# A hybrid encoder layer on one core: another PSUM bank for the first down accumulator, another order of down's first steps, and chunk 0's normalized inputs begun four items earlier

## The chip, the cores and the metric

The kernel runs on one core of one Trainium2 chip. The metric is the device time of one execution in microseconds (us). Engines are named as in the profile: PE (TensorE, matmuls), DVE (VectorE), ACT (ScalarE), POOL (GpSimd) and SP (SyncE, which here issues nearly all DMAs). Each engine has its own queue and works through it in order; between engines the instructions wait for each other by semaphores.

## The reference

One layer of a streaming encoder over 1056 tokens of width 1024 (1024 of a prompt, 32 of a sample). Cut to what matters here:

```python
h = rms_norm(x, g_mix);  z = h @ w_in          # q, k, v, conv and gates
a  = window_attn(q, k, v) @ w_attn_out
bo = (cb * conv) @ w_conv_out
x = x + (sigmoid(ga) * a + sigmoid(gb) * bo) @ w_mix_out
hc = rms_norm(x, g_cross)
co = softmax((hc @ w_cq) @ mem_k * s) @ mem_v   # cross attention, 256 memory tokens
x = x + co @ w_co
hm = rms_norm(x, g_mlp)
x = x + square(relu(hm @ w_up)) @ w_down        # hidden 4096
y = rms_norm(x, g_final)
```

All in float32.

## The kernel before, in words

Activations lie transposed: features on the 128 partitions (eight feature blocks f), tokens along the free axis in three chunks of 384, 384 and 288 tokens (chunks 0, 1, 2). Every float32 matmul is made of three fp32r products of split operands: high part times high part, high times low, low times high. `split` makes the parts: ACT casts the high part (L120), DVE subtracts to get the low part (L121). Where a gain belongs to it, ACT and DVE do it at L256 and L257.

*Weights.* `fetch_w` loads a raw weight tile of 128x1024 with a DMA on SP (L138, `wr`, two buffers), and `issue_w` splits it into `wh` and `wl` (three buffers each); two weights are split ahead of the one in use (`LOOK`). A kept weight has its low part loaded again from DRAM (L149) and only its cast made (L150). A usual item of the program is one weight against one chunk: 24 matmuls (`gemm`, L176 to L178) into one accumulator in PSUM.

*The trunk and what runs beside it.* `trunk(c)` is a list of 16 items of chunk c: eight `do_conv_out(c, f)` (it loads the attention branch from DRAM at L1075 and the gate at L1077, multiplies on DVE at L1080, adds at L1083 on POOL, on DVE for the last f, and splits the sum into M tiles), then eight `do_mix(c, f)` (L1093 loads x, L1097 adds it on DVE and so frees the accumulator). `beside(steps, fillers, late)` interleaves: item i of the fillers, then those of `late` that are due at i, then one step of the cross attention of the chunk before. `cross_steps(1)` are those steps for chunk 1: `do_cq`, then per head `scores` (reduce L1175, reciprocal L1178, scale L1180), `turn` (transposed probabilities, split) and `values` (L1210, L1211, L1217, L1219, L1222, L1223 give the Y tiles that `co` multiplies), then `do_co` in two halves of 24 matmuls each (L1236 to L1238, each result added to x at L1241).

*Normalized MLP inputs.* `normed_split(c, f)` makes the input of the up projection: DVE multiplies x by gain and the reciprocal root R (L1264) into a tile `ct`, SP stores it to DRAM (L1265, `xn_d`), ACT casts the high part (L1267), DVE subtracts the low part (L1268). The two DVE instructions are pinned in the order in which the program has them; others a scheduler orders, engine by engine, when the program is built. `ct` is a ring of six tiles that nearly all loads share. `normed(c, at)` puts the eight f at items at, at+1, ... of the fillers.

*Up and down.* The MLP over chunks 0 and 1 is computed by products over quadrants with sums and differences of operands (names b11, b21, n4, t2 and so on, 16 feature tiles each, stored in DRAM); chunk 2 is computed plainly (h2, two halves of 16 tiles). The last up pair (`up_pair`) ends with `dve.tensor_sub(h21, B, s1)` (L1419), the last read of its accumulator B. `open_down` (L1430 and following) closes the old PSUM pool and opens a new one, `ps2`, with six accumulators `acc` and two `pt` tiles, in the order in which they are first asked for.

`beside_two` runs down's first phase. Each of its steps (j, t) takes one weight: `prod` makes 24 matmuls of 384 columns against eight tiles of b11 into accumulator j, and `two` 24 of 288 columns against eight tiles of h2 into accumulator ("z", j); all in `part` (L1650 to L1652). With t = 0 they are tiles 0 to 7 (Y tiles for both), with t = 1 tiles 8 to 15 (M tiles for b11, H tiles for h2). Four j with two t are eight steps; `pump` loads the next operands between them (ring `ct`) and splits those that were loaded by the call before. `to_x1` (L1640) adds a finished accumulator to x; `refold` (L1479 to L1486) makes operands of later products on DVE.

Of the kernel before, what the change touches and what calls it, by code (L numbers as in the profile page):

```python
# [10 lines left out]
F32 = mybir.dt.float32  # L11
# [7 lines left out]
P = 128  # L19
# [19 lines left out]
def hybrid_step(ctx: ExitStack, tc: tile.TileContext, io):  # L39
# [5 lines left out]
    def nm(s):  # L45
        uid[0] += 1
        return f"{s}_{uid[0]}"

    def opened(name, **kw):
        cm = tc.tile_pool(name=name, **kw)  # L50
        return cm, cm.__enter__()

    def closed(cm):
        cm.__exit__(None, None, None)
# [7 lines left out]
    ps_cm, ps = opened("ps", bufs=1, space=PSUM)  # L62
# [46 lines left out]
    def item(fn, *keys):  # L109
        plan.append((fn, keys))  # L110
        worder.extend(keys)
# [126 lines left out]
    def chunk_stats(c):  # L238
        chunk_col(c)
        chunk_row(c)  # L240
# [1194 lines left out]
    def open_down():  # L1435
        nonlocal ps, n_acc
        closed(L["cm"])
        closed(ps_cm)
        H["pool"] = ctx.enter_context(tc.tile_pool(name="hpool", bufs=16, reuse_waits="tile"))
        ps = ctx.enter_context(tc.tile_pool(name="ps2", bufs=1, space=PSUM, reuse_waits="tile"))  # L1440
        n_acc = 6
        ps.tile([P, 384], F32, tag="pt", bufs=2, name=nm("pt"))

    def hslot(n):
        return H["pool"].tile([P, n], F32R, tag=f"H{n}", name=nm("H"))
# [43 lines left out]
    def cross_steps(c):  # L1489
        units = [Cross(c, h) for h in ([0, 1, 2, 3] if c < 2 else [4, 0, 1, 2, 3])]  # L1490
        nu = len(units)
        steps = [("call", [mem_load] if c == 0 else [mem_load_s])] if c < 2 else []
        steps.append(("call", [lambda: chunk_stats(c)]))
        steps.append(("items", [(do_cq(c, j), ("w_cq", j)) for j in range(2)]))
        for i in range(nu + 2):
            calls = []
            if i < nu:
                calls.append(units[i].scores)
            if 0 <= i - 2 < nu:
                calls.append(units[i - 2].values)  # L1500
            if 0 <= i - 1 < nu:
                calls.append(units[i - 1].turn)
            steps.append(("call", calls))
            if c < 2 and i < nu:
                steps.append(("call", []))
        if c == 1:
            steps.append(("call", []))
        if c == 2:
            steps.append(("call", [open_late]))
            steps.append(("call", []))  # L1510
            steps.append(("call", []))
        steps.append(("items", [(do_co(c, 0), ("w_co", 0))]))
        steps.append(("items", [(do_co(c, 1), ("w_co", 1))]))
        steps.append(("call", [lambda: chunk_stats(c)]))
        return steps

    def beside(steps, fillers, late=()):
        for i, filler in enumerate(fillers):
            item(*filler)
            for x in [x for at, x in late if at == i]:  # L1520
                item(lambda x=x: x())
            if steps:
                kind, what = steps.pop(0)
                for x in what:
                    if kind == "items":
                        item(*x)
                    else:
                        item(lambda x=x: x())
        return steps

    def trunk(c):
        return [(do_conv_out(c, f), ("w_conv_out", f)) for f in range(NF)] + [
            (do_mix(c, f), ("w_mix", f)) for f in range(NF)
        ]
# [4 lines left out]
    left = beside([], trunk(0))  # L1539
    left = beside(cross_steps(0), trunk(1))  # L1540

    normed = lambda c, at: [(at + f, lambda f=f: normed_split(c, f)) for f in range(NF)]
    left = beside(left + cross_steps(1), trunk(2), normed(0, 6))
    left = beside(left + cross_steps(2), up0(0) + up0(1), [(min(f + 1, NF - 1), x) for f, x in normed(1, 0)])
    assert not left
    for j in range(NF):
# [161 lines left out]
    steps = [(j, t) for j in range(4) for t in range(2)]  # L1708
# [13 lines left out]
    def twos(half, t):  # L1722
        return [h2_of(half, k) for k in range(8 * t, 8 * t + 8)]

    def beside_two(w, kind, then, half, f, begin, more=(), each=None):

        for n, (j, t) in enumerate(steps):
            if (j, t) == (3, 1) and more:
                item(lambda: wanted.__setitem__(slice(0, 0), more))

            def fn(ws, j=j, t=t, n=n):
                prod(kind, j, t, then)(ws)
                pump(pace(13 - 2 * n))
                if each:
                    each(n)
                two(half, j, t, f, begin)(ws)
                pump(pace(12 - 2 * n))

            item(fn, ("w_down", w, j, t))

    def alone(w, kind, then, begin=True, end=True, more=None):
        for j, t in steps:
# [6 lines left out]
            if more and (j, t) == (1, 0):  # L1749
                item(lambda: [pump(0), more()])  # L1750

    want(twos(0, 1), ops("b21"))
    beside_two(0, "b11", ((*C12, True, False), (*C21, False, False), (*C22, False, False), (*C11, True, False)), 0, 0, True,
               twos(1, 0), lambda n: n > 3 and refold(n - 4))
    want(twos(1, 1), ops("n4")[4:], ops("n4")[:4])
    beside_two(1, "b21", ((*C11, True, True),), 1, 0, False, each=lambda n: n < 5 and refold(n + 4))
    want(ops("t2"))
# [2 lines left out]
    for n, (j, t) in enumerate(steps):  # L1760
        then = ((*C12, False, False), (*C21, True, False), (*C22, True, False))
# [124 lines left out]
```

## Time and profile before

| | us |
|---|---|
| median of 3 runs | 1790.34 |
| lowest and highest | 1790.26, 1791.42 |
| the profiled execution itself | 1788.14 |
| its span, first to last instruction | 1786.3 |
| granted TensorE clock, mean | 0.992 of full |

A line of the timeline reads: start, duration, engine, line of the kernel, operation, out<-in by the names of tiles (without buffer numbers), shape, count of equal instructions in a row; in brackets how long the engine was idle before it and whose end released it. PE's weight load overlaps its matmuls (PEld). Matmuls are pipelined, so the distance of two starts is the cost of one, not the duration shown. A row of windows has the busy time of each engine in that stretch, and at the end the granted clock, the DMA engines' mean busy share and the GB/s moved.

### The profile page before, as it was taken

Reading aid. Unit: us, or ns where it says so; the run is one execution under the profiler, and the core shown is the slowest. Engines: PE = TensorE matmul, PEld = TensorE weight load, DVE = VectorE, ACT = ScalarE, POOL = GpSimd, SP = SyncE. Lnnn points to the kernel's source line nnn. Section 1 sums busy time; section 2 is a strip of 40 time slices with the busy share of each in tenths; the row PEclk is TensorE's granted clock in tenths of the full one; section 3 lists DMA queues with packets and bytes.
Section 4 is the critical chain, followed back from the end, with each engine's and each line's share of the span. In section 5 each row is a group of like instructions: output and inputs, shape, how many; then the busy total and the mean of one; then the engine's idle time right before and its main releaser. Section 6 shows DMA issues by size and latency. Waiting matters only on the chain.

```text
span 1786.3 us, 30138 instructions
## 1 busy us (share of the span) xinstructions
PE 1744.9 (98%) x11030; PEld 1722.1 (96%) x11030; DVE 1195.2 (67%) x2082; ACT 816.3 (46%) x1574; POOL 738.3 (41%) x777
## 2 busy tenths in 40 slices
PE   9999999999999999999999999999999899999997
PEld 8999999999999999999999989999999899999997
DVE  6767696767687767367666877776666666436674
ACT  8655565555332335144465755632222343324453
POOL 2256877874676744402324242375555300100112
PEclk9999999999999999999999999999999999999998
DMA  4424342424332437779766767744334596546672
GB/s 181 144 66 142 100 153 101 146 92 156 120 100 91 161 104 254 262 247 316 261 216 212 248 211 234 264 158 146 138 127 140 161 302 208 166 135 197 194 256 99
DMA packets 177973, 313.04 MB, mean 175 GB/s; under 512 B 18048, under 2 KB 137632, under 8 KB 177696
## 3 DMA queue, kind: packets, MB, share of 16 engines
q1 hardware_dynamic: 168176, 276.97, 46.8%
q0 software_dynamic: 9216, 33.56, 5.3%
q8 instruction: 87, 1.43, 0.3%
q14 instruction: 62, 0.51, 0.1%
q10 hardware_dynamic: 432, 0.58, 0.1%
HBM read 233.23 MB, written 77.81 MB: 174 GB/s over the span
## 4 chain that ended last, share of the span: by engine, by line
PE 81%; DMA 7%; DVE 5%; issue 3%; ACT 2%; POOL 2%; SPq 1%; POOLq 0%; DVEq 0%; ACTq 0%
PE acc L176 10%; PE acc L177 10%; PE acc L178 10%; PE acc L852 6%; PE acc L854 6%; PE acc L853 6%; PE acc L1651 5%; PE acc L1650 5%; PE acc L1652 5%; PE pa L177 2%; PE pa L176 2%; PE pa L178 2%; PE pt L577 2%; DVE wl L121 1%; PE sc L552 1%
## 5 line engine op out<-in xcount | busy, mean ns | idle before, releaser
L121 DVE TENSOR_TENSOR wl<-wr,wh 128x1024 fp32r<-128x1024 f32 (+1 forms) x224 | 313.6, 1401 | 102.5 <-ACT wh L120 101.2
L120 ACT CAST wh<-wr 128x1024 fp32r<-128x1024 f32 (+1 forms) x224 | 234.3, 1046 | 299.0 <-PE acc L1651 73.9
L253 POOL TENSOR_TENSOR xacc<-xacc,ct 128x384 f32<-128x384 f32 (+1 forms) x62 | 76.2, 1230 | 328.3 <-ACT ct L251 325.8
L176 PE MATMUL acc<-X,wh 128*128 128x384 f32 (+1 forms) x624 | 205.1, 329 | 0.6 <-ACT wh L120 0.6
L178 PE MATMUL acc<-Y,wl 128*128 128x384 f32 (+1 forms) x624 | 201.9, 324 | 1.8 <-DVE wl L121 1.8
L178 PE MATMUL acc<-X,wl 128*128 128x384 f32 (+1 forms) x624 | 203.3, 326 | 0.0
L177 PE MATMUL acc<-X,wh 128*128 128x384 f32 (+1 forms) x624 | 202.8, 325 | 0.4 <-DVE X L257 0.4
L176 PE MATMUL acc<-Y,wh 128*128 128x384 f32 (+1 forms) x624 | 202.0, 324 | 1.0 <-DVE ct L1024 0.7
L177 PE MATMUL acc<-Y,wh 128*128 128x384 f32 (+1 forms) x624 | 201.6, 324 | 0.0
L569 POOL TENSOR_SCALAR S<-S,rec 128x256 f32<-128x256 f32 (+1 forms) x132 | 124.8, 959 | 49.8 <-DVE rec L567 49.5
L1650 PE MATMUL acc<-Y,wh 128*128 128x384 f32 (+1 forms) x352 | 114.1, 324 | 6.5 <-DVE lt L1419 6.1
L177 PEld LDWEIGHTS acc<-X,wh 128*128 128x128 f32 x624 | 118.2, 189 | 2.3 <-DVE X L257 1.5
L176 PEld LDWEIGHTS acc<-X,wh 128*128 128x128 f32 x624 | 118.2, 189 | 2.1 <-ACT wh L120 0.8
L178 PEld LDWEIGHTS acc<-Y,wl 128*128 128x128 f32 x624 | 117.1, 188 | 3.1 <-DVE wl L121 3.1
L178 PEld LDWEIGHTS acc<-X,wl 128*128 128x128 f32 x624 | 118.1, 189 | 1.0 <-DVE wl L121 0.2
L176 PEld LDWEIGHTS acc<-Y,wh 128*128 128x128 f32 x624 | 117.0, 188 | 2.1 <-DVE ct L1024 1.0
L177 PEld LDWEIGHTS acc<-Y,wh 128*128 128x128 f32 x624 | 117.1, 188 | 0.0
L1651 PE MATMUL acc<-Y,wh 128*128 128x384 f32 (+1 forms) x352 | 113.9, 323 | 0.1
L1652 PE MATMUL acc<-Y,wl 128*128 128x384 f32 (+1 forms) x352 | 113.7, 323 | 0.0
L120 ACT CAST wh<-s 128x1024 fp32r<-128x1024 f32 x50 | 52.3, 1051 | 89.0 <-PE acc L853 52.2
L121 DVE TENSOR_TENSOR Y<-ct,Y 128x384 fp32r<-128x384 f32 (+1 forms) x128 | 70.7, 581 | 32.6 <-ACT Y L120 32.5
L120 ACT CAST Y<-ct 128x384 fp32r<-128x384 f32 (+1 forms) x128 | 59.6, 486 | 62.7 <-DMA ct<-bc_d 15.2
(359 smaller groups left out, 5231.5 us busy)
## 6 DMA issues: line engine op xcount, KB each, us to landing
wr<-in_w_in SPq DMA_DIRECT2D x55, 512.0 KB, 3.3
wr<-in_w_up SPq DMA_DIRECT2D x48, 512.0 KB, 3.8
wr<-in_w_down SPq DMA_DIRECT2D x32, 512.0 KB, 3.7
wr<-wsum_d SPq DMA_DIRECT2D x32, 512.0 KB, 3.5
wl<-wl_d SPq DMA_DIRECT2D x28, 512.0 KB, 4.7
wr<-in_w_conv_out SPq DMA_DIRECT2D x24, 512.0 KB, 4.9
wr<-in_w_mix SPq DMA_DIRECT2D x24, 512.0 KB, 4.5
xacc<-in_w_down POOLq DMA_DIRECT2D x20, 512.0 KB, 3.8
```

The lines of the kernel that those rows point to most:

```text
L120: act.copy(hi, src)
L121: dve.tensor_sub(lo, src, hi.bitcast(F32))
L176: pe.matmul(out, wh[:, a], hi, start=(k == 0), stop=False)
L177: pe.matmul(out, wh[:, a], lo, start=False, stop=False)
L178: pe.matmul(out, wl[:, a], hi, start=False, stop=(k == len(acts) - 1))
L569: pool_e.tensor_scalar_mul(stl[:, h, :nk], stl[:, h, :nk], rec[:, h : h + 1])
L852: pe.matmul(acc, wh[:, a], hi, start=(start and k == 0), stop=False, skip_group_check=True)
L853: pe.matmul(acc, wh[:, a], lo, start=False, stop=False, skip_group_check=True)
L854: pe.matmul(acc, wl[:, a], hi, start=False, stop=(k == 3), skip_group_check=True)
L1650: pe.matmul(a, wh[:, s], hi, start=(start and k == 0), stop=False, skip_group_check=True)
L1651: pe.matmul(a, wh[:, s], lo, start=False, stop=False, skip_group_check=True)
L1652: pe.matmul(a, wl[:, s], hi, start=False, stop=(stop and k == len(acts) - 1), skip_group_check=True)
```

## The change

Three edits.

1. `open_down` no longer asks for a `pt` tile first. So the accumulators come first in the new pool: the first one takes the bank that the old `pt` tile had (its last reader is L1292 on DVE), and no longer that of the last up pair's B. The third one takes B's.
2. The first `beside_two` gets its own list of steps: (0,0), (1,0), (0,1), (1,1) and then the rest as before. The second step so multiplies the second weight by the tiles that the first step has used, and M and H tiles come in at the third.
3. `normed(0, 6)` becomes `normed(0, 2)`: the eight `normed_split(0, f)` are issued beside items 2 to 9 of `trunk(2)` and not beside 6 to 13.

```diff
@@ open_down
         ps = ctx.enter_context(tc.tile_pool(name="ps2", bufs=1, space=PSUM, reuse_waits="tile"))
         n_acc = 6
-        ps.tile([P, 384], F32, tag="pt", bufs=2, name=nm("pt"))
@@
     normed = lambda c, at: [(at + f, lambda f=f: normed_split(c, f)) for f in range(NF)]
-    left = beside(left + cross_steps(1), trunk(2), normed(0, 6))
+    left = beside(left + cross_steps(1), trunk(2), normed(0, 2))
@@
-    def beside_two(w, kind, then, half, f, begin, more=(), each=None):
+    def beside_two(w, kind, then, half, f, begin, more=(), each=None, steps=steps):
         for n, (j, t) in enumerate(steps):
@@
     beside_two(0, "b11", ((*C12, True, False), (*C21, False, False), (*C22, False, False), (*C11, True, False)), 0, 0, True,
-               twos(1, 0), lambda n: n > 3 and refold(n - 4))
+               twos(1, 0), lambda n: n > 3 and refold(n - 4), [(0, 0), (1, 0), (0, 1), (1, 1)] + steps[4:])
```

Behind L1441 every line of the changed kernel stands one lower: its L1649 to L1651 are L1650 to L1652 of before, its L1639 is L1640, its L1485 is L1486.

Numbers behind a tile's name count buffers. PE's queue where the first step of down ends and the second begins, before (acc_3125 is the first z accumulator, wh_3077 the second weight, M tiles are b11 8 and following):

```order
L1650 MATMUL acc_3125_16442<-Y2_3086_16315,wh_3062_16254 128x288
L1651 MATMUL acc_3125_16442<-Y2_3087_16316,wh_3062_16254 128x288
L1652 MATMUL acc_3125_16442<-Y2_3086_16315,wl_3063_16255 128x288
L1650 MATMUL acc_3112_16393<-M_3099_16358,wh_3077_16296 128x384
L1651 MATMUL acc_3112_16393<-M_3100_16359,wh_3077_16296 128x384
L1652 MATMUL acc_3112_16393<-M_3099_16358,wl_3078_16297 128x384
```

The same place in the changed kernel:

```order
L1649 MATMUL acc_3124_16441<-Y2_3086_16315,wh_3062_16254 128x288
L1650 MATMUL acc_3124_16441<-Y2_3087_16316,wh_3062_16254 128x288
L1651 MATMUL acc_3124_16441<-Y2_3086_16315,wl_3063_16255 128x288
L1649 MATMUL acc_3140_16496<-Y0_3013_16023,wh_3077_16296 128x384
L1650 MATMUL acc_3140_16496<-Y0_3014_16024,wh_3077_16296 128x384
L1651 MATMUL acc_3140_16496<-Y0_3013_16023,wl_3078_16297 128x384
```

The second weight now meets b11 0 (Y0_3013 and its low part Y0_3014) in a third accumulator, where it met b11 8 (M_3099) in the first.

DVE's queue some 20 us later in the same phase, before: splits of the last h2 tiles (H, 128x288), a `refold` (L1486) and the low part of the fourth weight (wl_3140).

```order
L121 TENSOR_TENSOR H_3144_16530<-ct_3135_16485,H_3143_16529 128x288
L1486 TENSOR_TENSOR fold_3196_16780<-fold_3195_16778,fold_3196_16780 128x384
L121 TENSOR_TENSOR wl_3140_16494<-wr_3138_16491,wh_3139_16493 128x1024
L121 TENSOR_TENSOR H_3146_16534<-ct_3136_16487,H_3145_16533 128x288
L121 TENSOR_TENSOR H_3148_16538<-ct_3137_16489,H_3147_16537 128x288
```

And in the changed kernel:

```order
L121 TENSOR_TENSOR H_3144_16526<-ct_3134_16484,H_3143_16525 128x288
L1485 TENSOR_TENSOR fold_3195_16779<-fold_3194_16777,fold_3195_16779 128x384
L121 TENSOR_TENSOR H_3146_16530<-ct_3135_16486,H_3145_16529 128x288
L121 TENSOR_TENSOR wl_3139_16493<-wr_3137_16490,wh_3138_16492 128x1024
L121 TENSOR_TENSOR H_3148_16534<-ct_3136_16488,H_3147_16533 128x288
```

The fourth weight moved behind the seventh H tile and ahead of the eighth; on ACT its cast moved in the same way.

DVE's queue just ahead of co of chunk 1, before (L1264 and L1268 are `normed_split`, L1223 the last value that co waits for, L1241 the first additions of co's results):

```order
L1264 SCALAR_TENSOR_TENSOR ct_2253_11960<-Gb0_1765_9912,prm_72,R_2040_11076 128x384
L1211 TENSOR_TENSOR tO_2257_11972<-o_2256_11967,tO_2257_11972 64x384
L1097 TENSOR_TENSOR Gb2_2276_12061<-acc_2275_12036,xt_2274_12034 128x288
L257 SCALAR_TENSOR_TENSOR Y2_2266_12015<-Gb2_2264_12012,prm_72,Y2_2265_12014 128x288
L1264 SCALAR_TENSOR_TENSOR ct_2268_12021<-Gb0_1774_9954,prm_72,R_2040_11076 128x384
L1268 TENSOR_TENSOR Y0_2255_11964<-ct_2253_11960,Y0_2254_11963 128x384
L1223 TENSOR_TENSOR Y1_2166_11624<-tO_2257_11972,h0_2258_11976 64x384
L257 SCALAR_TENSOR_TENSOR Y2_2278_12064<-Gb2_2276_12061,prm_72,Y2_2277_12063 128x288
L1268 TENSOR_TENSOR Y0_2270_12025<-ct_2268_12021,Y0_2269_12024 128x384
L1241 TENSOR_TENSOR Ga1_1921_10574<-acc_2283_12076,Ga1_1921_10574 128x384
```

The same place in the changed kernel:

```order
L121 TENSOR_TENSOR wl_2264_11989<-wr_2262_11986,wh_2263_11988 128x1024
L257 SCALAR_TENSOR_TENSOR Y2_2257_11968<-Gb2_2255_11965,prm_72,Y2_2256_11967 128x288
L1211 TENSOR_TENSOR tO_2260_11979<-o_2259_11974,tO_2260_11979 64x384
L1097 TENSOR_TENSOR Gb2_2267_12019<-acc_2266_11994,xt_2265_11992 128x288
L1223 TENSOR_TENSOR Y1_2178_11652<-tO_2260_11979,h0_2261_11983 64x384
L1097 TENSOR_TENSOR Gb2_2276_12061<-acc_2275_12036,xt_2274_12034 128x288
L257 SCALAR_TENSOR_TENSOR Y2_2269_12022<-Gb2_2267_12019,prm_72,Y2_2268_12021 128x288
L257 SCALAR_TENSOR_TENSOR Y2_2278_12064<-Gb2_2276_12061,prm_72,Y2_2277_12063 128x288
L1241 TENSOR_TENSOR Ga1_1921_10574<-acc_2283_12076,Ga1_1921_10574 128x384
```

No `normed_split` row stands between the last values and the first addition of co any more; the last two stand ahead of the last two weights of the stretch.

## The prediction

> **What bounds the kernel now.** I read the page first.
>
> ```profile
> span 1786.3 us, 30138 instructions
> PE 1744.9 (98%) x11030; PEld 1722.1 (96%) x11030; DVE 1195.2 (67%) x2082; ACT 816.3 (46%) x1574; POOL 738.3 (41%) x777
> ```
>
> TensorE (PE) is busy 98% of the span. The matmuls themselves are not touched by the change, so it can gain only where PE stands idle or runs at a lowered clock. The second view is the list of PE's waits, sorted by their total (total, times, longest).
>
> ```profile
> PE acc L1650 <- DVE lt L1419: 6.1, 1, 6.1
> ...
> PE acc L1236 <- DVE Gb L1097: 1.6, 2, 1.4
> PE acc L1236 <- ACT Y L1217: 1.6, 2, 0.9
> ...
> PE acc L1651 <- DVE M L121: 0.5, 1, 0.5
> ```
>
> The longest wait of the kernel is the first matmul of the down projection. It waits for L1419, VectorE's last read of accumulator B, and no operand of it comes from there: it is a wait for a PSUM bank. The next place is co, the output projection of the cross attention (L1236). The changed lines touch both. Third, the timeline of PE at the start of down (start, duration, then the wait in brackets):
>
> ```profile
> 1424.43 0.34 PE L854 MATMUL acc<-Y,wl 128*128 128x384 f32 x1
> 1430.92 0.66 PE L1650 MATMUL acc<-Y,wh 128*128 128x384 f32 x1 [6.15 <-DVE lt L1419]
> ...
> 1435.19 0.34 PE L1651 MATMUL acc<-Y,wh 128*128 128x384 f32 x1
> ...
> 1440.30 0.34 PE L1650 MATMUL acc<-M,wh 128*128 128x384 f32 x1
> ...
> 1444.46 0.29 PE L1650 MATMUL acc<-H,wh 128*128 128x288 f32 x1
> ...
> 1447.66 0.34 PE L1650 MATMUL acc<-Y,wh 128*128 128x384 f32 x1
> ```
>
> From these rows: 24 matmuls of 384 columns take 4.16 us (0.173 each, 1440.30 to 1444.46), 24 of 288 take 3.20 (0.133 each), one step of down 7.36. The last matmul before down has its slot until 1424.60, so 1430.92 − 1424.60 = 6.32 us are empty. After that the clock is low: 13 spacings from 1430.92 to 1435.19 take 4.27 us where 13 × 0.173 = 2.25 would do, so 2.0 more are lost. Together 8.3 us.
>
> Fourth, windows of 10 us around co (busy us of PE, weight load, DVE, ACT, POOL, each with its count, then granted PE clock, DMA share, GB/s), and PE's timeline there:
>
> ```profile
> 980.00:990.00 10.00, 10.00 (x73) 10.00 (x72) 7.09 (x12) 7.41 (x13) 1.61 (x2) 1.00 0.76 241
> 990.00:1000.00 10.00, 10.00 (x79) 10.00 (x78) 6.89 (x17) 6.69 (x17) 2.31 (x3) 1.00 0.76 245
> ...
> 1020.00:1030.00 10.00, 9.81 (x72) 9.48 (x71) 10.00 (x18) 7.32 (x14) 4.46 (x3) 1.00 0.83 267
> 1030.00:1040.00 10.00, 7.84 (x27) 6.00 (x27) 8.36 (x14) 5.96 (x11) 7.66 (x8) 0.66 0.70 227
> ```
>
> ```profile
> 1028.90 0.33 PE L1236 MATMUL acc<-Y,wh 128*128 128x384 f32 x1
> ...
> 1031.97 0.44 PE L1236 MATMUL acc<-Y,wh 128*128 128x384 f32 x1 [1.41 <-DVE Gb L1097]
> ...
> 1033.57 1.33 PE L1236 MATMUL acc<-Y,wh 128*128 128x384 f32 x3 [0.61 <-ACT Y L1217]
> ...
> 1039.33 0.29 PE L176 MATMUL acc<-M,wh 128*128 128x288 f32 x1
> ...
> 1042.49 0.34 PE L1236 MATMUL acc<-Y,wh 128*128 128x384 f32 x1
> ...
> 1047.55 0.34 PE L176 MATMUL acc<-Y,wh 128*128 128x384 f32 x1
> ```
>
> Here DVE is the limit: full from 1020 to 1030, while it had about 3 us in 10 free from 980 to 1000. The first 24 matmuls of co take 1039.33 − 1028.90 = 10.43 us where 24 × 0.173 = 4.15 would do: 6.3 lost, partly at a granted clock of 0.66. The second 24 take 5.06: 0.9 lost.
>
> **The change part by part.** *Accumulator bank.* Removing the dummy `pt` tile puts the first accumulator of down on the bank that the old `pt` had. The timeline of DVE there:
>
> ```profile
> 1422.28 0.45 DVE L1292 SCALAR_TENSOR_TENSOR ct<-pa,R 128x288 f32<-128x288 f32 x1
> ...
> 1425.87 1.22 DVE L121 TENSOR_TENSOR wl<-wr,wh 128x1024 fp32r<-128x1024 f32 x1
> ...
> 1427.48 2.36 DVE L121 TENSOR_TENSOR Y<-ct,Y 128x288 fp32r<-128x288 f32 x4
> ...
> 1430.23 0.54 DVE L1419 TENSOR_TENSOR lt<-acc,s 128x384 f32<-128x384 f32 x1
> ...
> 1437.14 1.65 DVE L121 TENSOR_TENSOR M<-ct,M 128x384 fp32r<-128x384 f32 x3 [0.39 <-ACT M L120]
> ...
> 1444.79 1.22 DVE L121 TENSOR_TENSOR wl<-wr,wh 128x1024 fp32r<-128x1024 f32 x1
> 1445.93 1.75 DVE L121 TENSOR_TENSOR H<-ct,H 128x288 fp32r<-128x288 f32 x4
> ```
>
> The old bank is read last by L1292, until 1422.73, before PE needs it. So the first step can start at 1424.6 and end at 1432.0, all in full clock. Its second half, with h2 0–7 (Y, 288 columns), starts at 1428.8; the eighth of these is needed after 21 more spacings, 1428.8 + 21 × 0.133 = 1431.6, and its low part ends at 1429.84: in time. B's bank now belongs to the third accumulator, wanted at 1432.0; L1419 ends at 1430.77. If L1419 were 2 us later, the same wait would return there, shorter.
>
> *Step order.* With the bank alone, PE would come to b11 8–15 (M) at 1432.0, whose last low part ends at 1437.14 + 1.65 = 1438.8: some 6 us of waiting back. The new second step (1,0) takes the operands that are already there and the weight split at 1425.87–1427.1. It runs 1432.0 to 1439.3, and covers the loads of M. M then runs 1439.3 to 1443.5, and h2 8–15 (H) from there, the eighth wanted at 1443.5 + 21 × 0.133 = 1446.3. The timeline of ACT:
>
> ```profile
> 1442.53 1.04 ACT L120 CAST wh<-wr 128x1024 fp32r<-128x1024 f32 x1
> 1444.66 1.90 ACT L120 CAST H<-ct 128x288 fp32r<-128x288 f32 x4 [1.09 <-DMA ct<-hid_d]
> ```
>
> The seventh and eighth H come at 1444.66, released by their load. In the new order the fourth weight's cast (1.04) stands between them on ACT, and its DVE part (1.22) ahead of the eighth's low part: 1444.66 + 0.47 + 1.04 + 0.47 = 1446.6 for the cast, then the weight's low part until 1447.4 or so, then 0.44 more: about 1447.8, a stall of about 1.3 us behind 1446.3 that was not there before. Bounds: 0 if the loads come earlier, 2.5 if the load is as late and the weight also waits. The fifth and sixth weights have lost two steps' slack in part; I take 0.5 for them, 0 to 1.5. Sum of both edits: −8.3 + 1.3 + 0.5 = **−6.5** (−4.3 to −8.3).
>
> What a short stall costs beside itself: after 6.15 us of idling PE was slow for 4.27 us; in co, where no gap was longer than 1.41, the granted clock was 0.66 as well. So a leftover stall of 1.3 may bring up to the same 2.0 of slow matmuls; with it the lower end is −2.3. The Trainium skill, "TensorE: Matmul & The Clock Gate", Part 1, says that the clock drops only after an idle window of about 3.4 us and comes back after about as much sustained work; the 6.15 us case agrees with it, the co rows do not, and by it the stall would cost its own 1.3 alone.
>
> *Chunk 0's normalized MLP inputs earlier, `normed(0, 2)` for `normed(0, 6)`.* Each of eight blocks is a DVE multiply (L1264), an ACT cast (L1267), a DVE subtraction (L1268) and a store on SP (L1265). No work is added; six blocks move ahead of the mix phase, into the stretch where DVE had 3 of 10 us free. The late rows of DVE before:
>
> ```profile
> 1030.06 1.02 DVE L1264 SCALAR_TENSOR_TENSOR ct<-Gb,prm,R 128x384 f32<-128x384 f32 x1
> ...
> 1032.27 0.60 DVE L1264 SCALAR_TENSOR_TENSOR ct<-Gb,prm,R 128x384 f32<-128x384 f32 x1
> 1032.80 1.01 DVE L1268 TENSOR_TENSOR Y<-ct,Y 128x384 fp32r<-128x384 f32 x1
> 1034.08 0.80 DVE L1223 TENSOR_TENSOR Y<-tO,h 64x384 fp32r<-64x384 f32 x1 [0.28 <-ACT h L1222]
> ...
> 1035.65 1.15 DVE L1268 TENSOR_TENSOR Y<-ct,Y 128x384 fp32r<-128x384 f32 x1
> ```
>
> 1.02 + 0.60 + 1.01 + 1.15 = 3.8 us of DVE go from between the last operations that co waits for (L1097, L1223). Of co's 6.3 lost, 2.0 are the two waits named above; most of the rest is slow clock that follows from them. If L1223 comes 2.6 earlier (three rows stand ahead of it) and the clock stays up, 2.6 plus some 2 to 3 of slow matmuls go: −5. The 0.9 of the second 24 stays. Against it stands the load of the conv branch, whose tile ring the new blocks share:
>
> ```profile
> 1004.59 0.46 DVE L1083 TENSOR_TENSOR sgl<-sgl,ct 128x288 f32<-128x288 f32 x1 [0.16 <-DMA ct<-m_d]
> ```
>
> That load now comes later in SP's queue; L1083 may wait 0 to 2 us on DVE, with the queue of DVE behind it, and PE has the mix matmuls' first blocks to cover that. I count it in the range: **−5** (−1 to −7).
>
> Sum: −6.5 − 5 = −11.5. The profiled execution took 1788.14, 2.2 below the median of the runs shown; it becomes 1776.6, and the median 1790.34 becomes 1778.8. Both gains last, since PE is the bound on both sides of each place.
>
> **The rivals.**
>
> *DVE only shifts its delay.* DVE's queue is in order, and the stretch from 980 to 1036 is not empty. If the early blocks push softmax and M splits back, co waits as before and B gives −1.5: −8, 1782.3. For it: DVE full at 1020–1030. Against it: the 3 free us in 10 before 1000.
>
> *Down is bound by its loads.*
>
> ```profile
> 1430.00:1440.00 10.00, 9.08 (x46) 9.12 (x47) 5.98 (x12) 4.13 (x9) 1.00 (x1) 0.74 0.99 337
> ```
>
> The DMA share is 0.99 there. M, H and the weights then come no earlier than before, PE waits at later steps for what it ran ahead of, and the 8.3 shrinks to 3: −8, 1782.3. For it: the casts wait for loads. Against it: in the list of waits down has, beside the first, none over 0.5 us, so there is slack to eat.
>
> *The bank wait changes its name.* Some other thing of the first step (a weight, an operand) holds PE till about 1430: only −5, 1785.3. Against it: the weight and Y rows above.
>
> *Slower: stores in SP's queue.* All eight stores wait in the same in-order queue as the weight fetches.
>
> ```profile
> L1265 SPq DMA_DIRECT2D xn_d<-ct x8: 319/326/422, 1001.6 to 1033.4; - x8
> ...
> DMA to landing us min/median/max: 1.8/4.5/5.8
> ```
>
> A store cannot be issued before its L1264 is done; what stands behind it, the fetch of the next mix weight, waits too. If the six moved stores each held a weight 2 us or more beyond PE's slack, 6 × 2 = 12 us would come on the path and B's −5 be lost: 12 − 6.5 = +5.5, 1795.8. It decides from 6.5 / 6 = 1.1 us each. Against it: an issue takes 0.33 us, and two weights are split ahead of use.
>
> **How the numbers follow.** Forecast as summed 0.52, DVE shift 0.20, loads 0.15, bank wait renamed 0.06, stores 0.05, and 0.02 for no gain at all. The predicted time is 1778.8. The range must reach from −15.3 (both ends of the bounds, 1775.0, and 1 for the spread of 1.2 us among the runs shown) to the case of the renamed wait: 1774 to 1786. Faster or slower counts from 0.2% (3.6 us), about what a measurement of this kernel can tell from no change. Faster: nearly all of the first four cases, 0.88; same: their low ends and the last, 0.07; slower: 0.05.
>
> **What would show it.** Right: the 6.1 us wait for L1419 is gone, the second step starts near 7.4 us after the first, a wait of 1 to 2 us for an H or a weight stands some 20 us into down; the first 24 co matmuls take 5 to 6 us with the granted clock near 1.0 in that window, and DVE is busier from 980 to 1000. Wrong: PE waits for M, H or weights of more than 4 us in down; co still starting with waits for L1097 or L1217 and a clock of 0.66; or waits for weights at L176 between 1000 and 1030.

## The result and the profile after

| | median us (runs) | lowest to highest |
|---|---|---|
| before | 1791.32 (5) | 1790.26 to 1795.09 |
| changed | 1785.37 (5) | 1782.46 to 1787.10 |

The ratio is 0.9963, 95% interval [0.9948, 0.9979]: 0.37% faster, some 6.5 us by the means and 5.95 by the medians. The direction and the range held; 11.5 us had been forecast, and 1785.37 lies 0.6 us inside the slow end of 1774 to 1786. One execution of a later experiment (e7, 2854.96 us) stands far above all others and is left out of its ratio. The profiled execution of the changed kernel took 1785.85 us, with this span:

```profile
span 1784.1 us, 30120 instructions
PE 1744.3 (98%) x11030; PEld 1721.8 (97%) x11030; DVE 1195.0 (67%) x2082; ACT 814.3 (46%) x1574; POOL 735.1 (41%) x777
```

PE's list of waits after (total, times, longest):

```profile
PE acc L1651 <- DVE wl L121: 2.0, 3, 0.8
...
PE acc L176 <- ACT M L120: 1.1, 1, 1.1
PE acc L1236 <- DVE Ga L1241: 1.1, 2, 0.9
...
PE acc L1650 <- DVE H L121: 0.9, 1, 0.9
```

The wait of 6.1 us for L1419 and the waits of co for L1097 are gone. New are short waits for weight low parts (L1651 here is L1652 of before), for an H tile, for an M tile and, where 0.2 us stood before, for L1241's Ga. In PE's timeline at the start of down:

```profile
1426.61 0.34 PE L854 MATMUL acc<-Y,wl 128*128 128x384 f32 x1
1426.79 0.33 PE L1649 MATMUL acc<-Y,wh 128*128 128x384 f32 x1
...
1449.73 0.40 PE L1650 MATMUL acc<-H,wh 128*128 128x288 f32 x1 [0.90 <-DVE H L121]
...
1458.66 0.44 PE L1651 MATMUL acc<-Y,wl 128*128 128x384 f32 x1 [0.64 <-DVE wl L121]
...
1481.68 0.44 PE L1651 MATMUL acc<-M,wl 128*128 128x384 f32 x1 [0.56 <-DVE wl L121]
...
1490.11 0.45 PE L1651 MATMUL acc<-H,wl 128*128 128x384 f32 x1 [0.78 <-DVE wl L121]
```

Down follows up without a gap, but it starts at 1426.8, not at 1424.6: the changed kernel is 2.2 us *later* there. That comes from before any changed instruction. So the two spans cannot be subtracted; the executions are compared stretch by stretch. The borders are the starts of matmuls that all kernels have: the last of co of chunk 0 (L1238), the last of co of chunk 1, the last of up (L854) and PE's last. Ahead of the first border nothing is changed.

| stretch, us | before | changed |
|---|---|---|
| start to co of chunk 0 | 958.2 | 960.5 |
| to co of chunk 1 (edit 3 acts here) | 89.2 | 87.6 |
| to the last matmul of up | 377.1 | 378.5 |
| to PE's last matmul (edits 1, 2) | 353.9 | 349.5 |

So edit 3's stretch gave 1.5 us and down 4.4 in this pair of traces; the first row's 2.3 against it is no work of the change.

Inside the two stretches I count PE's lost time: the distance of each two starts, less 0.173 us for a matmul of 384 columns and 0.133 for one of 288. Between the two co, 8.9 us were lost before and 7.4 after. In the 18 us of co (65 to 83 us behind the border) the loss fell from 6.2 to 1.9, and in the 25 us ahead of it, where conv_out ends and mix begins, it rose from 0.5 to 3.2. PE's timeline has the new waits there:

```profile
1008.58 0.54 PE L176 MATMUL acc<-M,wh 128*128 128x288 f32 x2 [1.10 <-ACT M L120]
...
1019.93 0.40 PE L176 MATMUL acc<-M,wh 128*128 128x288 f32 x1 [0.39 <-ACT wh L150]
...
1031.76 0.45 PE L1236 MATMUL acc<-Y,wh 128*128 128x384 f32 x1 [0.62 <-ACT wh L120]
...
1038.96 0.44 PE L1236 MATMUL acc<-Y,wh 128*128 128x384 f32 x1 [0.90 <-DVE Ga L1241]
```

The windows over co show that the clock stayed up after (1.00, where 0.66 stood before):

```profile
1020.00:1030.00 10.00, 10.00 (x75) 9.97 (x76) 9.79 (x17) 7.43 (x13) 5.64 (x5) 1.00 0.82 271
1030.00:1040.00 10.00, 8.48 (x55) 7.93 (x54) 8.70 (x14) 6.91 (x12) 7.44 (x6) 1.00 0.79 278
```

Why co waits less shows on ACT. L1217 makes a Y tile of co from DVE's sum (L1211). ACT's timeline, before and then in the changed kernel:

```profile
1031.93 1.05 ACT L150 CAST wh<-wr 128x1024 fp32r<-128x1024 f32 x1 [0.30 <-DMA wr<-in_w_co]
1033.01 0.51 ACT L1217 CAST Y<-tO 64x384 fp32r<-64x384 f32 x1
```
```profile
1034.21 0.51 ACT L1217 CAST Y<-tO 64x384 fp32r<-64x384 f32 x1 [1.50 <-DVE tO L1211]
...
1035.16 1.04 ACT L150 CAST wh<-wr 128x1024 fp32r<-128x1024 f32 x1
```

Before, L1217 stands in ACT's queue behind the cast of a kept weight (L150), which waits for its load, and starts 1.5 us after the end of L1211. In the changed kernel it stands ahead of that cast and starts at once. L1211 itself ends no earlier: 73.3 us behind the border before, 73.7 after. PE's order has moved too: in the changed kernel 22 matmuls of a mix item (2.9 us) stand behind co's first two, where before all 24 of co's first half stand in a row.

### The profile page after: what moved, and what is told of

The parts are those of the page before. It is cut to its first block, busy times and chain, and to the rows that moved or that the text cites. A ratio compares the mean times of both kernels' runs of the same rounds, so it can differ in the third digit from the quotient of the medians.

```text
span 1784.1 us, 30120 instructions
## 1 busy us (share of the span) xinstructions
PE 1744.3 (98%) x11030; PEld 1721.8 (97%) x11030; DVE 1195.0 (67%) x2082; ACT 814.3 (46%) x1574; POOL 735.1 (41%) x777
## 4 chain that ended last, share of the span: by engine, by line
PE 76%; DMA 9%; DVE 5%; ACT 3%; issue 3%; POOL 2%; SPq 1%; POOLq 0%; DVEq 0%; ACTq 0%
PE acc L176 10%; PE acc L177 10%; PE acc L178 10%; PE acc L852 6%; PE acc L854 6%; PE acc L853 6%; PE acc L1651 4%; PE acc L1650 4%; PE acc L1649 4%; PE pa L177 2%; PE pa L176 2%; PE pa L178 2%; DVE wl L121 2%; PE pt L577 2%; ACT wh L120 1%
## 5 line engine op out<-in xcount | busy, mean ns | idle before, releaser
L176 PE MATMUL acc<-X,wh 128*128 128x384 f32 (+1 forms) x624 | 205.2, 329 | 1.0 <-ACT wh L120 1.0
L176 PE MATMUL acc<-Y,wh 128*128 128x384 f32 (+1 forms) x624 | 202.5, 325 | 2.7 <-DVE ct L1292 1.8
L176 PEld LDWEIGHTS acc<-Y,wh 128*128 128x128 f32 x624 | 117.7, 189 | 3.6 <-DVE ct L1292 2.0
L176 PEld LDWEIGHTS acc<-X,wh 128*128 128x128 f32 x624 | 118.2, 189 | 2.5 <-ACT wh L120 1.2
L1651 PE MATMUL acc<-Y,wl 128*128 128x384 f32 (+1 forms) x352 | 113.1, 321 | 0.6 <-DVE wl L121 0.6
L1650 PE MATMUL acc<-Y,wh 128*128 128x384 f32 (+1 forms) x352 | 113.1, 321 | 0.2 <-DVE Y L121 0.2
L1649 PE MATMUL acc<-Y,wh 128*128 128x384 f32 (+1 forms) x352 | 113.1, 321 | 0.0
L121 DVE TENSOR_TENSOR Y<-ct,Y 128x384 fp32r<-128x384 f32 (+1 forms) x128 | 71.1, 585 | 28.4 <-ACT Y L120 28.1
```

The lines of the kernel that those rows point to most:

```text
L121: dve.tensor_sub(lo, src, hi.bitcast(F32))
L176: pe.matmul(out, wh[:, a], hi, start=(k == 0), stop=False)
L1649: pe.matmul(a, wh[:, s], hi, start=(start and k == 0), stop=False, skip_group_check=True)
L1650: pe.matmul(a, wh[:, s], lo, start=False, stop=False, skip_group_check=True)
L1651: pe.matmul(a, wl[:, s], hi, start=False, stop=(stop and k == len(acts) - 1), skip_group_check=True)
```

## The experiments

All ratios are to the kernel before, in runs on the same chip (e1 to e4 on one, e5 to e8, e9 to e11 and e12 on three others); "lost" is PE's lost time as above, from one profile each.

| kernel | ratio, 95% interval | co to co, us (lost) | last of up to PE's last, us (lost in its first 95) |
|---|---|---|---|
| before | 1 | 89.2 (8.9) | 353.9 (8.4) |
| changed | 0.9963 [0.9948, 0.9979] | 87.6 (7.4) | 349.5 (4.1) |
| e1, edit 1 | 0.9992 [0.9981, 1.0003] | 88.5 (8.2) | 354.7 (9.4) |
| e2, edit 2 | 1.0005 [0.9995, 1.0015] | 89.7 (9.5) | 353.0 (8.1) |
| e3, edits 1, 2 | 0.9964 [0.9952, 0.9976] | 90.2 (10.0) | 349.3 (3.2) |
| e4, edit 3 | 0.9994 [0.9985, 1.0002] | 87.9 (7.7) | 354.8 (8.8) |
| e5, three steps ahead | 0.9974 [0.9963, 0.9984] | 90.5 (10.3) | 348.3 (3.2) |
| e6, own ring | 0.9967 [0.9955, 0.9980] | 86.1 (5.8) | 350.1 (3.9) |
| e7, stores on ACT | 0.9964 [0.9952, 0.9975] | 87.0 (6.7) | 351.1 (5.6) |
| e8, start 4 | 0.9983 [0.9974, 0.9993] | 93.2 (13.0) | 349.2 (3.1) |
| e9, no fold loads | 0.9968 [0.9955, 0.9981] | 89.9 (9.7) | 346.3 (0.5) |
| e10, ring and ACT | 0.9973 [0.9963, 0.9983] | 87.1 (6.9) | 350.5 (5.0) |
| e11, changed again | 0.9968 [0.9955, 0.9981] | 87.6 (7.4) | 352.4 (5.1) |
| e12, start 3 | 0.9951 [0.9936, 0.9966] | 86.4 (6.2) | 349.1 (3.0) |

**e1, the bank alone.**

```diff
-        ps.tile([P, 384], F32, tag="pt", bufs=2, name=nm("pt"))
```

> Edit 1 alone (first down accumulator on the old pt bank; steps and normed as before). Theory, the bank and the step order work only together: the 6.1 us wait for L1419 is gone, but PE then meets M and H tiles that are no earlier than before; the last H low part of the second step was done at about 1446.8 in the trace of before and PE ended that step at 1447.7, so 0.5 to 1.5 us are gained and waits of some 6 us for M and H tiles stand in the second step. Rival, the bank wait alone was the loss: 6 to 8 us faster, no wait of over 1 us in the second step.

No difference that can be told. The wait for L1419 is gone, and PE meets late tiles in the second step instead. Its timeline in that step (not all waits), and two windows (PE, weight load, DVE, ACT, POOL; then the granted clock):

```profile
1435.05 0.44 PE L1649 MATMUL acc<-M,wh 128*128 128x384 f32 x1 [1.13 <-ACT M L120]
...
1444.72 0.40 PE L1649 MATMUL acc<-H,wh 128*128 128x288 f32 x1 [0.53 <-ACT H L120]
1445.98 0.40 PE L1650 MATMUL acc<-H,wh 128*128 128x288 f32 x1 [0.86 <-DVE H L121]
```

```profile
1430.00:1440.00 10.00, 8.38 (x39) 6.55 (x38) 5.46 (x11) 3.55 (x7) 0.99 (x1) 0.87 0.94 313
1440.00:1450.00 10.00, 8.46 (x39) 7.15 (x38) 7.62 (x15) 7.32 (x14) 0.00 (x0) 0.84 0.93 285
```

The waits with a name come to 3.0 us, but 9.4 are lost: between them PE runs at the pace of the tiles, and at a lowered clock. The theory holds in the main, though less of the loss has a name than the 6 us it expected; the rival that the bank alone was the loss falls.

**e2, the step order alone.**

```diff
-               twos(1, 0), lambda n: n > 3 and refold(n - 4))
+               twos(1, 0), lambda n: n > 3 and refold(n - 4), [(0, 0), (1, 0), (0, 1), (1, 1)] + steps[4:])
```

> Edit 2 alone (down's first steps (0,0), (1,0), (0,1), (1,1); bank and normed as before). Theory, the two work only together: PE still waits about 6 us for L1419, and the new order covers loads that were in time anyway: no difference within 1 us. Rival, the loads of M and H were a limit by themselves: 2 to 4 us faster.

No difference, and the old wait at the head of the list of waits:

```profile
PE acc L1650 <- DVE lt L1419: 6.1, 1, 6.1
```

**e3, both.** The edits of e1 and e2, `normed(0, 6)` as before.

> Edits 1 and 2 without edit 3. Theory, what the changed kernel gained comes from here: about 4 us faster (8.3 us of wait and slow clock gone, some 3 to 4 us of new short waits for H and for weight low parts in down's first eight steps). The sum of the prediction: 6.5 us faster. Rival, the gain is edit 3's: no more than 2 us.

0.9964, as much as the whole change. Neither edit gives anything measurable by itself, together they give nearly all: one takes the wait away, the other what would come in its place. PE's waits with a name from 1420 to 1510 us are three, 1.6 of the 3.2 us lost there:

```profile
PE acc L1650 <- DVE H L121: 0.9, 1, 0.9
PE acc L1649 <- ACT Y L120: 0.4, 1, 0.4
PE acc L1651 <- DVE wl L121: 0.3, 1, 0.3
```

The H here is one at 1503.8, far behind the start; at 22 us into down, where the changed kernel waited 0.9 for an H tile, e3 waits for nothing.

**e4, the normalized inputs alone.**

```diff
-    left = beside(left + cross_steps(1), trunk(2), normed(0, 6))
+    left = beside(left + cross_steps(1), trunk(2), normed(0, 2))
```

> Edit 3 alone (normed(0, 2)). Theory from the trace of the changed kernel: the stretch from the first co of chunk 0 to 1073 us was 1.8 us shorter, since the clock stayed up in co but new waits for M (1.1), for weights (0.4 and 0.6) and for L1241 (0.9) came; so 0 to 2 us faster. The sum of the prediction: 5 us faster, with no such new waits. Rival, the stores in SP's queue hold up weights and the conv branch's load: as slow as before or up to 2 us slower.

In the time, 0.06% with an interval across 1. In the trace, 1.3 us in its stretch, with the same new waits as in the changed kernel:

```profile
1010.43 0.54 PE L176 MATMUL acc<-M,wh 128*128 128x288 f32 x2 [0.60 <-ACT M L120]
...
1041.36 0.44 PE L1236 MATMUL acc<-Y,wh 128*128 128x384 f32 x1 [1.05 <-DVE Ga L1241]
```

And a surprise in the built order. ACT's queue at the fourth weight of down, with edit 3 alone and with edits 1 and 2 alone:

```
edit 3 alone                                      edits 1 and 2 alone
H_3141_16525<-ct_3134_16483 128x288               H_3141_16521<-ct_3133_16482 128x288
H_3143_16529<-ct_3135_16485 128x288               H_3143_16525<-ct_3134_16484 128x288
H_3145_16533<-ct_3136_16487 128x288               wh_3138_16492<-wr_3137_16490 128x1024
wh_3139_16493<-wr_3138_16491 128x1024             H_3145_16529<-ct_3135_16486 128x288
H_3147_16537<-ct_3137_16489 128x288               H_3147_16533<-ct_3136_16488 128x288
```

The weight behind the seventh H tile comes with edit 3, whose instructions stand 400 us earlier, and not with the order of the steps: an edit there has reordered a queue here. It is this form of edit 3 that does it: the traces of e6, e10 and e11 have the order of the left column, those of e7, e8 and e12 that of the right.

**e5, one more step ahead** (edits 1 and 2, edit 3 left out).

```diff
+    [(0, 0), (1, 0), (2, 0), (0, 1), (1, 1), (2, 1)] + steps[6:]
```

> Edits 1 and 2 with one more step ahead, edit 3 left out: (0,0), (1,0), (2,0), (0,1), (1,1), (2,1), then the rest. From the last matmul of up to PE's last, 353.0 to 354.8 us passed without both edits and 349.3 to 349.5 with both. Theory, the rest of the 8.3 us is lost in waits for tiles and weights that are loaded late: one more step on loaded tiles puts M and H 7.4 us later, so no wait for H is left, waits for weight low parts of about 0.5 to 0.9 remain, and the stretch is 348 to 349 us, the whole 0.5 to 1 us faster than edits 1 and 2. Rival, the loads are only moved and PE waits as much for weights instead: 349 to 350, no difference from edits 1 and 2. Slower if the third z accumulator finds its bank held: one new wait in the third step, 350 to 352.

The stretch is 348.3, as the theory had it, but 3.2 us are lost in its first 95 us as in e3, a wait of 0.8 for an H tile stays, and the time is not below e3's. The 1.0 us less than e3 lies behind the 95 us, in the scatter that e11 shows. So the rival is nearer: the loss is only moved.

**e6 to e8** ask what the new wait for an M tile is.

```diff
 e6, normed_split (chunk 0)
-        t = tmp(CH[c][1])
+        t = cr.tile([P, CH[c][1]], F32, tag="nt", bufs=1, name=nm("nt"))
 e7, normed_split (chunk 0)
-        sp.dma_start(xn_d[c][:, f], t)
+        act.dma_start(xn_d[c][:, f], t)
 e8
-    ... normed(0, 2))
+    ... normed(0, 4))
```

> All three edits, and the eight normed_split tiles of chunk 0 in a ring of their own (one buffer) instead of the shared ring ct. From the last co matmul of chunk 0 to that of chunk 1 88.5 to 90.2 us passed in four traces without edit 3, 87.6 and 87.9 with it. Theory, the shared ring holds back the conv branch's loads, which is the new wait for an M tile (1.1 and 0.6 us): it is gone here, and the stretch is 86.3 to 87.0. Rival, the stores in SP's queue hold them back: the wait for M stays. Against it could work that one buffer makes the multiply of the next block wait for the landing of the store before: then DVE has new waits of 1 to 4 us in the conv phase and the stretch is 87.5 or more.

> All three edits, and the eight stores of chunk 0's normalized inputs issued from ACT's queue instead of SP's. Rival theory, SP's in-order queue: the stores hold weight fetches and the conv branch's loads, so the new waits for M (1.1, 0.6) and for the kept weight's cast (0.4) go, and the stretch from co of chunk 0 to co of chunk 1 is 86 to 87 us. Ring theory: the load still waits for its tile in ct, the wait for M stays within 0.5 to 1.2 and the stretch is 87.4 to 88.2.

> All three edits with normed(0, 4) instead of normed(0, 2). Theory, a trade between two losses: two blocks more are left in the mix phase, so co loses more (2 to 4 us after its first matmul instead of 2.0), while the conv branch's loads come two items earlier and the wait for M (1.1) goes: the stretch stays at 87 to 88.5, the whole as with all three edits within 1 us. Rival, the co wait falls away as soon as the last block stands ahead of the last mix weights: 86 to 87, 1 us faster.

In e6 and in e7 the wait for M is gone; in e7 that for the kept weight grew from 0.4 to 0.9, and e6 has a new one of 0.5 for DVE (L1180). What POOL waited for the conv branch's loads (L1083, from 980 to 1012 us) tells more than PE does; the list of waits of before, of the changed kernel, of e7 and of e6:

```profile
POOL sgl L1083 <- DMA ct<-m_d: 5.5, 1, 5.5
```
```profile
POOL sgl L1083 <- DMA ct<-m_d: 29.8, 5, 8.8
```
```profile
POOL sgl L1083 <- DMA ct<-m_d: 24.8, 4, 9.2
```
```profile
POOL sgl L1083 <- DMA ct<-m_d: 16.4, 2, 9.3
```

POOL is not what bounds here (41% busy); the lists show what came last for it. With the stores off SP's queue the loads are hardly earlier: the last is issued 42.3 us behind the border, 43.5 in the changed kernel (40.8 before). With a ring of their own it is issued at 28.1. So the shared ring of six spaces the loads, as the theory had it; that e7 lost the wait for M all the same was not what the theory expected, and what of it is due to the queue and what to loads that landed sooner (at most 5.1 us, 6.2 in the changed kernel) stays open. Neither is faster in the time than the changed kernel.

In e8 the theory of a trade fell: two items later is not as good but much worse, 93.2 us. Co waits in one place longer than before the change, and ACT's timeline has why:

```profile
PE acc L1236 <- ACT Y L1217: 4.0, 1, 4.0
```
```profile
1040.32 1.04 ACT L150 CAST wh<-wr 128x1024 fp32r<-128x1024 f32 x1 [3.45 <-DMA wr<-in_w_co]
...
1041.82 0.51 ACT L1217 CAST Y<-tO 64x384 fp32r<-64x384 f32 x1
```

It is the order of before, with L1217 behind the kept weight's cast, and here that cast waits 3.45 us for its load. The traces without edit 3 have it as well: e1, e2, e3, e5 and e9 wait 1.87, 2.80, 0.68, 2.85 and 3.25 us for L1217, which starts 1.4 to 3.9 us after the end of L1211; with start 2 and 3 in the shared ring and the stores on SP (changed, e4, e11, e12) it starts within 0.6, and PE waits for it in none.

**e9, fewer transfers in down** (edits 1 and 2; the kernel leaves out refold's sixteen loads and fills their tiles with zeros, so some of down's operands hold no data).

```diff
-                    sp.dma_start(fold[k], op_d[k][:, step // 2])
+                    pool_e.memset(fold[k], 0.0)
```

> Edits 1 and 2 without edit 3, and the sixteen loads of refold (192 KB each, 3.1 of the 19.5 MB that move from 1430 to 1500 us) left out: its tiles are set to zero on POOL, so 16 of the 64 sum operands of down are wrong. DVE's subtractions and the stores stay. In the first 95 us from the last matmul of up, 3.15 us are lost in the kernel with edits 1 and 2 (8.4 before), nearly all between 52 and 76 us. Theory, down is now bound there by its transfers: with 16% fewer bytes in that stretch most of the loss goes, 0.3 to 1.2 us are left, and the stretch from the last matmul of up to PE's last matmul is 346 to 348 us (349.3 with edits 1 and 2). Rival, DVE's queue (the subtractions ahead of the weight's low part) or the order of the queues: 2.5 to 3.5 us stay lost, 349 to 350.

0.5 us are lost in the first 95 us of down, where e3 loses 3.2. The ratio, 0.9968, is no better than e3's: in the time the 3 us don't show. The windows from 1480 to 1510 of e3 and then of e9:

```profile
1480.00:1490.00 10.00, 9.72 (x61) 9.40 (x62) 6.59 (x13) 1.05 (x1) 0.00 (x0) 1.00 0.68 216
1490.00:1500.00 10.00, 9.50 (x59) 9.06 (x58) 7.38 (x17) 3.00 (x7) 0.00 (x0) 1.00 0.85 275
1500.00:1510.00 10.00, 9.10 (x60) 8.86 (x59) 5.84 (x11) 6.42 (x13) 0.00 (x0) 1.00 0.68 226
```
```profile
1480.00:1490.00 10.00, 10.00 (x68) 10.00 (x67) 7.90 (x17) 5.96 (x13) 0.00 (x0) 1.00 0.82 247
1490.00:1500.00 10.00, 10.00 (x65) 10.00 (x64) 5.12 (x9) 4.95 (x10) 0.00 (x0) 1.00 0.67 218
1500.00:1510.00 10.00, 10.00 (x70) 10.00 (x69) 4.31 (x6) 3.09 (x6) 0.00 (x0) 1.00 0.35 105
```

PE is full, and the transfers are done earlier (a DMA share of 0.35 in the last row, 0.68 with the loads). So PE, 8 us ahead of its old time, ran into the transfers of this phase, and that is where the rest of the 8.3 went. Whether by the bytes alone or by DVE's queue standing behind a subtraction that waits for its load, e9 doesn't separate: it takes both away. For the waits for weights the trace of the changed kernel does: it is the queue. DVE ahead of the wait at 1481.68:

```profile
1479.93 0.56 DVE L1485 TENSOR_TENSOR fold<-fold,fold 128x384 f32<-128x384 f32 x1 [2.36 <-DMA fold<-b_d]
1480.41 1.22 DVE L121 TENSOR_TENSOR wl<-wr,wh 128x1024 fp32r<-128x1024 f32 x1
```

In the built order this weight's cast is the one that ACT ended at 1471.69, nearly 9 us earlier; its low part came late because it stands behind `refold`'s subtractions, which waited for their loads. The weight of 1490.11 stands behind another such wait, of 3.22. The late Y and H tiles of e3 are another matter: there ACT's casts wait for their own loads.

**e10, e6 and e7 together.**

> All three edits, chunk 0's normalized tiles in a ring of their own and their stores on ACT's queue. Between the co of chunk 0 and that of chunk 1 PE lost 7.4 us in the changed kernel, 5.8 with the own ring, 6.7 with the stores on ACT (8.2 to 10.3 without edit 3). Theory, what held the conv branch's loads were the stores ahead of them in SP's queue, which both versions undo: together 5.3 to 6.0 lost, no wait for M. Rival, ring and queue are two causes that add up: 4.5 to 5.2. In the time, 0 to 2 us below the changed kernel.

Neither: 6.9 lost, and a wait for M of 1.4 came back. The trace points to another cause, named as a danger for e6. DVE's timeline:

```profile
1006.98 0.62 DVE L1264 SCALAR_TENSOR_TENSOR nt<-Gb,prm,R 128x384 f32<-128x384 f32 x1 [2.42 <-DMA xn_d<-nt]
1007.52 0.45 DVE L1083 TENSOR_TENSOR sgl<-sgl,ct 128x288 f32<-128x288 f32 x1
```

The one buffer makes L1264 wait for the landing of the store before, and the last conv sum (L1083 on DVE) stands behind it.

**e11, the changed kernel once more.**

> The changed kernel once more, on the same chip as the two others. Theory: the same 0.35% below before, within 0.12%; the two stretches that the edits touch as in its first trace within 0.5 us (87.6 and 349.5 us), while what lies ahead of them (0 to 960 us) differs by up to 5 us between executions without any edit. Rival, a part of the difference found belonged to that execution: the stretches differ by over 1 us.

The time agrees (0.9968), and so does the stretch between the co (87.6). Down's does not: 352.4 against 349.5. Of the 2.9, 1.0 lie in the first 95 us, and 1.6 in one wait for an M tile 320 us in, which is 0.5 in the trace of before and 1.0 in e4's. So one trace places a gain in down only within some 3 us: by this one it would be 1.5, not 4.4. The ratios over many runs carry the verdicts on edits 1 and 2. Over all traces the picture holds: down took 353.0 to 354.8 us in the four without both edits, 348.3 to 352.4 in the nine with them (e9 left out); co to co took 88.5 to 90.5 in the six without edit 3, 87.6 to 87.9 in the three with it as it is.

**e12, start 3.**

```diff
-    ... normed(0, 2))
+    ... normed(0, 3))
```

> All three edits with normed(0, 3). In the changed kernel the fourth weight's cast stands behind seven H casts on ACT, and so it does with edit 3 alone; with edits 1 and 2 alone it stands behind six, and so here. Theory, the wait for an H tile 22 us into down and the next one for a weight (0.9 and 0.6) are edit 3's work by that order: here no wait for H within 25 us of the last matmul of up, and 2.8 to 3.8 us lost in the first 95 us (4.1 and 5.1 in two traces of the changed kernel, 3.15 with edits 1 and 2). Rival, the wait for H comes from the loads, which differ between executions: a wait of 0.5 to 1.5 for H there, 4 to 5 lost. In the stretch from co of chunk 0 to co of chunk 1: 87.6 with start 2, 93.2 with start 4; 88 to 91 is expected with 3. In the time within 2 us of the changed kernel.

3.0 us are lost, as was expected. The waits for H 22 us in are smaller but not gone (two of 0.2, with 0.9 lost around them); what is gone is the wait for a weight 32 us in. PE's waits from 1420 to 1510:

```profile
PE acc L1651 <- DVE wl L121: 1.4, 1, 1.4
PE acc L1650 <- DVE H L121: 0.2, 1, 0.2
PE acc L1649 <- ACT H L120: 0.2, 1, 0.2
```

So the loss 22 us in does not hang on the order alone: with the weight behind seven H tiles 1.0 to 1.6 us are lost there (changed, e6, e10, e11), behind six none in e3, e5 and e8, but 0.4 in e9, 0.9 here and 1.3 in e7. The loss 32 us in does go with the order: 0.9 to 1.6 in all four of the first, nothing in the six others.

Between the co, 86.4 us are better than the 88 to 91 expected: no wait for M, and co as good as with start 2. The ratio 0.9951 is the lowest of all; its interval overlaps that of the changed kernel, so it is below before for certain and below the changed kernel only by appearance.

## Why the prediction was right or wrong

The direction was right, and the mechanism of edits 1 and 2 was. That the time fell inside the range was in part luck: its slow end was set by the rival of the renamed wait, which did not come, and the gain was about half of the sum.

*The bank wait, 6.3 empty and 2.0 at a low clock.* Right: all of it is gone where down starts (changed, e3), and all of it stays without the bank (e2, e4).

*"With the bank alone ... some 6 us of waiting back."* Right in kind, too small in size: more than 6 came back, for e1 loses 9.4 us where 8.4 were lost. It is not one wait, though, but PE at the pace of its tiles.

*The new second step covers the loads of M.* Right: no wait for M or anything else in the first 22 us (changed), 59 us (e3).

*"A stall of about 1.3 us" for the eighth H.* The size was nearly right (a wait of 0.9 in the changed kernel and in e11); its own terms, 1447.8 − 1446.3, make 1.5. The cause was given wrongly: I put the weight's new place to the new order of steps, and e4 and e3 show that edit 3 brings it. Nor does the wait for H need that place (e7, e12).

*"The fifth and sixth weights ... I take 0.5."* This is the step that failed in down: the fifth weight costs 0.8, within the bound, but then come 0.7 and 1.0 more 54 and 62 us in. I looked for late operands only over six steps, as if PE's lead would be absorbed there; it is spent against the transfers of the first 75 us (e9), by way of DVE's queue behind `refold`. With it the sum of edits 1 and 2 is 8.4 − 4.1 = 4.3 in the changed kernel and 5.3 in e3, not 6.5. That is the rival "down is bound by its loads" in part: it priced the gain at 3.

*The low clock after a short stall, "up to the same 2.0".* Not paid: the isolated waits of 0.9 and 0.6 in the changed kernel left the granted clock at 1.00:

```profile
1440.00:1450.00 10.00, 9.10 (x61) 8.89 (x60) 6.85 (x14) 6.57 (x15) 0.00 (x0) 1.00 0.93 288
1450.00:1460.00 10.00, 9.36 (x60) 9.04 (x59) 6.59 (x14) 3.81 (x8) 0.00 (x0) 1.00 0.96 300
```

*Edit 3, −5.* This is the term that was most off. Co itself lost 4.3 less (6.2 to 1.9), near the 5 of the sum, but not by the way that was summed. I let L1223 come 2.6 earlier because three rows of DVE ahead of it go; but the row that I showed has it waiting for ACT (L1222), and so it does after. DVE's L1211 came no earlier. What changed is that ACT's L1217 no longer stands behind the cast of a kept weight, which the prediction does not consider; L1223, released by ACT both times, came 1.1 earlier. So it is luck that 4.3 comes near 5. No run moves that cast alone, so how much of the 4.3 is its work, and how much that of the 22 mix matmuls, stays open.

The side cost, put at 0 with a bound of 2, was 2.7 (0.5 to 3.2), for an M tile and for kept weights. Whether it is a price of its own is not shown: in all 14 traces the last matmul of co comes 12.7 to 14.5 us after that L1217, so a late M may only move a wait. Net 1.5 in the trace; the time of edit 3 alone cannot be told from no change. By their items four blocks, not six, cross from mix to conv_out.

Edit 3 also seems to cost in down what the moved order costs there: 3.9, 4.1, 5.0 and 5.1 lost in the traces with it, 3.0 to 3.2 in four without, though 5.6 in e7, also without, most of that one wait for a weight and a low clock behind it. It would explain why edits 1 and 2 alone are as fast as all three; between so few traces that is argued, not shown. The rival "DVE only shifts its delay" had priced edit 3 at −1.5, which is what the trace gave, and L1211 bears it out; but co did not wait as before.

*The rivals "bank wait renamed" and "slower".* The first was e1's outcome, not the change's. The second didn't come: PE waited 1.0 us in all for weights between the co (0.4 and 0.6), where more than 6.5 would have been needed. The sign that the prediction gives for it, waits for weights at L176 between 1000 and 1030, did come, with the one of 0.4.

## What to carry to other kernels

A wait for a buffer that hides a wait for data is worth nothing until both go: price each edit alone and together, and expect the sum only from the pair. When the bound engine moves ahead by several us, ask not only for the next operand but how long its suppliers keep up: here the lead was half spent within 75 us. Where a scheduler orders the queues, an edit in one phase can reorder another; compare the built orders edit by edit, on every engine, before you put a stall or a gain down to one of them.

## What the runs showed that was not expected

The granted clock fell without a long idle gap. In e1 no wait in the second step was over 1.13 us, and the clock was 0.87 and 0.84 in the windows from 1430 to 1450; in co before the change it was 0.66 with gaps up to 1.41. With single waits of 0.6 to 0.9, 9 us apart, it stayed at 1.00, and so it did over the 4 us behind single waits of 1.42 (e12) and 1.63 (e11). Behind one wait of 2.01 in e7, for the weight 63 us into down, it did not; the 4 us from its end:

```profile
1490.00:1494.00 4.00, 3.99 (x14) 3.99 (x15) 3.30 (x7) 0.08 (x1) 0.00 (x0) 0.57 0.79 253
```

The Trainium skill, "TensorE: Matmul & The Clock Gate", Part 1, ties the drop to an idle window of about 3.4 us. By these rows a loosely filled stretch of a few us or a single gap of 2.0 does it as well, and the measurement decides.

Executions with the same instructions up to the co of chunk 0 reach it after 958.2 to 963.4 us, over 5 us apart: nearly as much as the change gives. That is why the stretches were compared and not the spans.
